# A decoder block on one core: softmax rows divided by VectorE, bias rows fetched from GpSimd's queue, and the sums of down's weights moved to other stages

## The chip, the core and the metric

The kernel runs on one core of a Trainium2 chip. The core has a matrix engine (TensorE, PE in the profile; its weight loads are a row of their own, PEld), VectorE (DVE), ScalarE (ACT), GpSimd (POOL) and SyncE (SP). Each works through a queue of its own in order and waits on semaphores for the others. Transfers are issued from the queues of SyncE, ScalarE and GpSimd. The metric is the device time of one execution in microseconds (us), the median of several runs; a single profiled execution gives the trace.

## The reference

One layer of a decoder block for 512 tokens of width 1024, all in float32:

```python
h = rms_norm(x, norm1_g) * (1 + scale1) + shift1          # shift, scale, gate = silu(c) @ ada_w + ada_b
q, k, v, p, g_attn, g_pool = split(h @ w_in)
q, k = rms_norm(heads(q)), rms_norm(heads(k))             # 8 heads of 64
attn = softmax(q @ k.T / 8 + bias[h, distance], causal) @ v
pool = (multiscale_pool(p) @ pool_w) * pool_scale         # trailing means over 2, 4, 8, 16 tokens
merged = sigmoid(g_attn) * (attn @ w_branch_attn) + sigmoid(g_pool) * (pool @ w_branch_pool)
x = x + gate1 * (merged @ w_out)
h2 = rms_norm(x, norm2_g) * (1 + scale2) + shift2
u_g, u_v = split(causal_dwconv3(h2 @ w_up))               # 2 x 2816 channels
x = x + gate2 * ((silu(u_g) * u_v) @ w_down)
```

With 512 tokens, blocks of 256 and three blocks to choose, the sparse attention selects every past block, so it is plain causal attention. The bias depends on the distance of query and key alone.

## The kernel before

**Precision.** Every float32 factor is split into a rounded part and a remainder (`hi`, `lo`: a ScalarE copy, then a VectorE subtraction), and each product is three matmuls (`mm3`, lines 131 to 134): hi by hi, hi by lo, lo by hi. So a weight tile of 128x1024 that arrives by DMA (`load_unit`, L81, a ring of five tiles issued by SyncE) costs one ScalarE copy (L113) and one VectorE subtraction (L123 or L1043) before TensorE can use it; `ahead` does this two units in advance.

**Order.** The queues of TensorE, VectorE and ScalarE run in the order of the program text. SyncE's and GpSimd's are ordered by the framework's planner, by the program's order and by when a tile's memory is free. Most tiles are 128x512 and come from one pool of 72 slots.

**Stages, in the order in which they run.** x is normalised and transposed; p and q, then k and v are projected; the eight heads run with the sixteen gate projections between them; the branches (A for attention, B for pooling, merged by the sigmoids of the gates); out; up with its convolution, 22 pairs of channel tiles; down.

**The heads (lines 785 to 808).** TensorE alternates: transposes of head h's softmax rows (`flip`, PT), logits of head h + 1 (S, L592 and L593), five steps of a gate, stacks of Q or K for a later head (T, L549), values of head h (O, L644), then more gate steps. Around it, in program order:

- `logits(h + 1)`: VectorE adds the bias to S and takes the row minimum in one pass (L601) for the four query tiles of 512, 384, 256 and 128 keys; ScalarE takes the exponential with the row sum (L605). The bias tile `trev` (128x512) is fetched from a small table `fd` in DRAM, row p shifted by p (`trev_get`, L578, ScalarE's queue). The fetch for head h + 1 is issued behind the exponentials of head h.
- `softmax`: VectorE's reciprocal (L616), then ScalarE multiplies the row tile by it (L617).
- `stacks`: ScalarE and VectorE in turn copy and split Q or K (L556, L557, L564, L565).
- `values`: ScalarE's `bot` (L651) and VectorE's `at` (L652) add the halves of O.
- `ada_col(2, h)` and `ada_col(3, h)`: one VectorE pass each over a 128x1024 tile (L206) for one column of a modulation vector.
- `t_get(h)` and `t_do(h - 1)`: see below.
- the splits of the gates' weights and of PT (L218, L219); O needs PT_l, the remainder of PT.

`pooling(3)` stands in head 5, its ScalarE split (`pool_h`, L218) in front of the evacuation of the next gate (L499).

**The sums of down's weights.** Down is done with seven products in place of eight, which need four sums of the weight blocks b11, b12, b22, b21. They are made ahead, in eleven sets kk = 0 to 10: `t_load` fetches four 128x512 blocks (L756, SyncE), `t_forms` adds them with four VectorE instructions (L761 to L764) and stores the four sums to DRAM (`tsum`, L766, GpSimd's queue), from where down loads them (`raw_t`). Sets 0 to 6 are added in heads 1 to 7, set 7 in the branches (L848), set 8 at pair 2 of up, sets 9 and 10 at pairs 20 and 21 (`T_AT`, L1132).

**Branches and out.** For j = 0 to 7: the branch weights (`br`), B and A, the sigmoids, `mg` = merged split by L218 and L219, and the split of out's weights, whose remainders GpSimd subtracts (L219, `wo_l`). Out adds to x per token tile t: `out_post` (L896, L897, with x fetched by GpSimd, L888), `out_norm` (L191 to L907, `xn`), transposes `hT` (L870), then h2 split into `h2h` and `h2l` (L877 to L880).

**Up.** The first four weight tiles run in two halves of the tokens (lines 1134 to 1141). `h_forms` makes sums of h2 for the pairs in `SEVEN` (even pairs 4 to 18), which also use seven products; the others use `up_mm`. `behind(0)` is the convolution of the pair before (L944 to L946), `behind(1)` its silu and product (L960, L967). `ka`, `kb`, `wg` (L1108) are ScalarE copies that TensorE waits for before it goes on in the same bank. `ada_col(5, k)` stands at the eight pairs of `ADA_AT`.

Of the kernel before, what the change touches and what calls it, by code (L numbers as in the profile page):

```python
# [15 lines left out]
P = 128  # L16
S = 512
D = 1024
H = 8
# [36 lines left out]
def block_kernel(tc, x, cvec, ada, wtok, wch, pool_w, wbr, wout, wup, wdn, pack, table, out):  # L56
# [4 lines left out]
    with ctx:  # L61
# [11 lines left out]
        def slot(name, dt=F32, w=512):  # L73
            return sp.tile([P, w], dt, tag="s", name=name)
# [494 lines left out]
        ath, atl = [], []  # L569
        apair = {}  # L570

        trevs = {}

        def trev_get(h):

            trevs[h] = slot(f"trev_{h}")
            fsrc = fd[h : h + 1, :]
            nc.scalar.dma_start(  # L578
                trevs[h], bass.AP(tensor=fsrc.tensor, offset=fsrc.offset, ap=[[1, P], [1, 512]]))

        def logits(h):

            ta = trevs.pop(h)[:, :]
            pss = []
            for qt in (3, 2, 1, 0):
                n = max((qt + 1) * P, 256)
                if qt:
                    sb = bank(f"S_{h}_{qt}")
                    sps = sb
                else:  # L590
                    sps = sb[:, 256:]
                nc.tensor.matmul(sps[:, :n], Q[h][:, tslice(qt)], K2[h][:, :n], start=True, stop=False)  # L592
                nc.tensor.matmul(sps[:, :n], Q[h][:, tslice(qt)], K1[h][:, :n], start=False, stop=True)  # L593
                pss.append(sps)
            rows, sms = [], []
            for i, qt in enumerate((3, 2, 1, 0)):
                n = (qt + 1) * P
                L = slot(f"L_{h}_{qt}")
                mn = mini.tile([P, 1], F32, tag="mn", name=f"mn_{h}_{qt}")
                rev = bass.AP(tensor=ta.tensor, offset=ta.offset + n - 1, ap=[list(ta.ap[0]), [-1, n]])  # L600
                nc.vector.tensor_tensor_reduce(  # L601
                    out=L[:, :n], in0=pss[i][:, :n], in1=rev, op0=ALU.add, op1=ALU.min, scale=1.0,
                    scalar=3e38, accum_out=mn)
                sm = mini.tile([P, 1], F32, tag="sm", name=f"sm_{h}_{qt}")
                nc.scalar.activation(L[:, :n], L[:, :n], AF.Exp, scale=-1.0, bias=mn, accum_out=sm)  # L605
                rows.append(L)
                sms.append(sm)
            if h + 1 < H:
                trev_get(h + 1)
            return rows, sms  # L610

        def softmax(h, rows, sms):
            for i, qt in enumerate((3, 2, 1, 0)):
                n = (qt + 1) * P
                ri = mini.tile([P, 1], F32, tag="ri", name=f"ri_{h}_{qt}")
                nc.vector.reciprocal(ri, sms[i])  # L616
                nc.scalar.activation(rows[i][:, :n], rows[i][:, :n], AF.Copy, scale=ri)  # L617
            return rows[::-1]


# [84 lines left out]
        fill(kgen, 3)  # L705
        pooling(0)
        pooling(1)
        fill(kgen, 4)
        qn = head_norm(qps, qr, "q")
        fill(kgen, 4)  # L710
# [3 lines left out]
        fill(kgen, 1)  # L714
        for g in range(2):
            pool_proj(g)
        fill(kgen, 3)
        fill(kgen, 2)
        fill(kgen, 100)
# [3 lines left out]
        vps = [bank(f"v_{t}") for t in range(TT)]  # L723
        vgen = tok_proj(2, vps, "v")
        fill(vgen, 3)
        fill(vgen, 4)
        kn = head_norm(kps, kr, "k")
        fill(vgen, 1)
        stacks(0, True)
        fill(vgen, 2)  # L730
        trev_get(0)
        stacks(1, True)
        stacks(0, False)
        fill(vgen, 5.5)
        rows = logits(0)
        fill(vgen, 2)
# [19 lines left out]
                nc.sync.dma_start(b[nm], wdn[plain[nm], i][:, u * 512 : u * 512 + 512])  # L756
            return b

        def t_forms(kk, b):
            i, u = divmod(kk, 2)  # L760
            nc.vector.tensor_add(b["b11"], b["b11"], b["b12"])  # L761
            nc.vector.tensor_add(b["b12"], b["b12"], b["b22"])
            nc.vector.tensor_add(b["b22"], b["b22"], b["b11"])
            nc.vector.tensor_add(b["b21"], b["b21"], b["b22"])  # L764
            for n, nm in (("t1", "b11"), ("t3", "b12"), ("t2", "b22"), ("t4", "b21")):
                nc.gpsimd.dma_start(tsum[n, i][:, u * 512 : u * 512 + 512], b[nm])  # L766

        tb = {}

        def t_get(kk):  # L770
            tb[kk] = t_load(kk)

        def t_do(kk):
            t_forms(kk, tb.pop(kk))

        gates = {}

# [7 lines left out]
        for h in range(H):  # L785
            pt = flip(h, rows)
            if h + 1 < H:
                rows = softmax(h + 1, *logits(h + 1))
            fill(gg, 3)
            if h % 2 == 0 and h < 6:  # L790
                stacks(h // 2 + 1, False)
            elif h in (1, 3):
                stacks((h + 3) // 2, True)
            values(h, *pt)
            ada_col(2, h)
            t_get(h)
            if h:
                t_do(h - 1)
            if h == 5:
                pooling(3)  # L800
            if h == 6:
                pool_proj(3)

            fill(gg, 3 if h < 5 else (share - 3) / 2)
            if h < 5:
                ada_col(3, h)
            fill(gg, (share - 3) / 2)
# [17 lines left out]
        for j in range(8):  # L825
# [18 lines left out]
            a, b = split_act(gp, f"mg_{j}")  # L844
            mgh.append(a)
            mgl.append(b)
            if j == 1:
                t_do(7)  # L848
            if j == 6:
                g1 = row_of(2, "g1")  # L850

# [57 lines left out]
        for t in range(TT):  # L909
            for f in range(2):  # L910
                if (t, f) == (0, 0):
                    for t_ in range(2):
                        for f_ in range(2):
                            out_mm(t_, f_, 0, KT - 2)
                if (t, f) != (3, 0):
                    out_mm(t, f, KT - 2 if t < 2 else 0, KT)
                    out_post(t, f, ops[t, f])
                if late:
                    ada_col(4, late.pop(0))
                    if not late:  # L920
                        nc.vector.scalar_tensor_tensor(acol[:, 32:40], acol[:, 32:40], 1.0, pk[:, C_N2 : C_N2 + 8],
                                                       op0=ALU.add, op1=ALU.mult)
            out_norm(t)
            if t == 2:
                out_mm(3, 0, 0, KT)
                out_post(3, 0, ops[3, 0])
                flip_h2(1)
# [200 lines left out]
            keep(ug[:, R], X)  # L1128
            return ug, uv

        ADA_AT = [4, 6, 8, 10, 12, 14, 16, 18]
        T_AT = [2, 20, 21]  # L1132
        first = []
        for i in range(4):
            ahead(f"up{i}", min(2, 2 * PLAIN - 1 - i))
            first.append((ready.pop(f"up{i}"), bank(f"u_{i}")))
            up_mm(first[i][1], first[i][0], 0, 256)
            if i == 1:
                flip_h2(3)
        for w, ps in first:  # L1140
            up_mm(ps, w, 256, 512)
        pend, summed = [], []
        S_AT = [3, 7, 11, 18]

# [13 lines left out]
        for j in range(NP):  # L1158
# [24 lines left out]
                behind(1)  # L1183
            pend.append((j, *u))
            if j + 1 in T_AT:
                t_get(8 + T_AT.index(j + 1))
            if j in T_AT:
                t_do(8 + T_AT.index(j))
            for k in range(8):
                if ADA_AT[k] == j:  # L1190
                    ada_col(5, k)
        behind(0)
        behind(1)


        g2 = row_of(5, "g2")
# [167 lines left out]
```

## Time and profile before

| | us |
|---|---|
| median of 3 runs (lowest, highest) | 701.92 (701.43, 702.06) |
| profiled execution | 704.26 |
| its span, first to last instruction | 702.0 |

Stages in the trace (us from the span's start): the heads with the gates about 109 to 252, branches 252 to 303, out 303 to 348, up 348 to 590, down to the end. In the profile's rows, "out<-in" are the tiles written and read, L123 is a line, and the text after "<-" in brackets names what ended the idle time of that engine. Times of a stretch are busy times of each engine; the granted clock is that of TensorE, 1.00 for full speed.

### The profile page before, as it was taken

What the parts mean: (1) busy time and instruction counts of PE and PEld (TensorE: products, weight loads), DVE (VectorE), ACT (ScalarE), POOL (GpSimd) and SP (SyncE); (2) the same over time, 40 slices, a digit from 0 to 9 for tenths busy, and PEclk for the clock granted to TensorE, in tenths of its full rate; (3) what the DMA queues carried; (4) which work ended last, traced back from release to release, by engine and by line L of the source; (5) the groups of instructions that cost most, each with busy time, mean ns of one, the idle gap of its engine ahead of it and who ended that gap; (6) DMA issues with size and microseconds to landing.
All of it is one profiled execution on the core that took longest, in us unless ns stands there. A gap on an engine that the chain in (4) does not pass through costs nothing.

```text
span 702.0 us, 9585 instructions
## 1 busy us (share of the span) xinstructions
PE 667.8 (95%) x3403; PEld 566.2 (81%) x3403; DVE 562.2 (80%) x922; ACT 380.7 (54%) x663; POOL 88.0 (13%) x117
## 2 busy tenths in 40 slices
PE   8999999988896897999999899999999999999997
PEld 6778788867675786788897789998889988788885
DVE  7887866676767779886659999898998897978774
ACT  8454546756663744640555555565655643867430
POOL 2003120011111134461300100000000011001000
PEclk9999999999999899999999999999999999999999
DMA  8875232666667499678323444234243397577751
GB/s 351 312 262 187 92 106 89 200 243 216 235 239 262 166 211 264 229 228 312 136 89 107 150 142 128 101 141 150 90 145 127 124 218 263 184 237 261 249 189 59
DMA packets 41830, 131.52 MB, mean 187 GB/s; under 512 B 5315, under 2 KB 5484, under 8 KB 41782
## 3 DMA queue, kind: packets, MB, share of 16 engines
q1 hardware_dynamic: 34694, 109.77, 45.7%
q0 software_dynamic: 5936, 19.04, 9.1%
q10 hardware_dynamic: 1152, 2.10, 0.8%
q8 instruction: 26, 0.43, 0.2%
q14 instruction: 22, 0.18, 0.1%
HBM read 115.13 MB, written 15.76 MB: 186 GB/s over the span
## 4 chain that ended last, share of the span: by engine, by line
PE 66%; DVE 17%; ACT 9%; issue 5%; DMA 2%; SPq 0%; ACTq 0%; DVEq 0%
PE u L133 6%; PE u L132 6%; PE u L134 6%; DVE raw_ada L206 3%; PE X L139 2%; PE X L140 2%; PE X L138 2%; PE uX L138 2%; PE uX L140 2%; PE uX L139 2%; PE o L134 2%; PE o L133 2%; PE o L132 2%; DMA raw_p<-in_wtok 2%; ACT L L605 2%
## 5 line engine op out<-in xcount | busy, mean ns | idle before, releaser
L132 PE MATMUL u<-h2h,hi_up 128*128 128x512 f32 (+1 forms) x256 | 93.1, 364 | 1.0 <-ACT hi_up L113 1.0
L134 PE MATMUL u<-h2h,lo_up 128*128 128x512 f32 (+1 forms) x256 | 92.9, 363 | 0.5 <-DVE lo_up L1043 0.5
L133 PE MATMUL u<-h2l,hi_up 128*128 128x512 f32 (+1 forms) x256 | 92.9, 363 | 0.0
L206 DVE CUSTOM_DVE_ANT_0 raw_ada<-raw_ada,cbc,pk 128x1024 f32<-128x1024 f32 x48 | 61.7, 1294 | 4.9 <-DMA raw_ada<-in_ada 2.8
L132 PEld LDWEIGHTS u<-h2h,hi_up 128*128 128x128 f32 x256 | 48.4, 189 | 8.7 <-ACT hi_up L113 1.4
L134 PEld LDWEIGHTS u<-h2h,lo_up 128*128 128x128 f32 x256 | 48.3, 189 | 8.5 <-DVE lo_up L1043 1.0
L133 PEld LDWEIGHTS u<-h2l,hi_up 128*128 128x128 f32 x256 | 48.4, 189 | 7.1
L132 PE MATMUL gate_ps<-h_h,hi_gate 128*128 128x512 f32 x128 | 52.1, 407 | 0.0
L133 PE MATMUL gate_ps<-h_l,hi_gate 128*128 128x512 f32 x128 | 51.6, 403 | 0.0
L134 PE MATMUL gate_ps<-h_h,lo_gate 128*128 128x512 f32 x128 | 51.6, 403 | 0.0
L766 POOL DMA_DIRECT2D tsum_t<-b x44 | 24.0, 546 | 205.2 <-DVE b L761 200.1
L605 ACT ACTIVATE L<-L,mn 128x512 f32<-128x512 f32 (+3 forms) x32 | 17.6, 551 | 33.5 <-DVE mn L601 21.0
L113 ACT ACTIVATE hi_t<-raw_t 128x1024 fp32r<-128x1024 f32 (+1 forms) x24 | 23.7, 988 | 17.5 <-PE Y L140 8.4
L123 DVE TENSOR_TENSOR lo_t<-raw_t,hi_t 128x1024 fp32r<-128x1024 f32 (+1 forms) x24 | 26.6, 1131 | 8.0 <-ACT hi_t L113 7.9
L113 ACT ACTIVATE hi_up<-raw_up 128x1024 fp32r<-128x1024 f32 x28 | 29.3, 1049 | 4.3 <-PE u L133 4.3
L1043 DVE TENSOR_TENSOR lo_up<-raw_up,hi_up 128x1024 fp32r<-128x1024 f32 x22 | 26.8, 1220 | 3.7 <-ACT hi_up L113 3.7
L134 PEld LDWEIGHTS gate_ps<-h_h,lo_gate 128*128 128x128 f32 x128 | 25.1, 196 | 5.6
L132 PEld LDWEIGHTS gate_ps<-h_h,hi_gate 128*128 128x128 f32 x128 | 25.5, 199 | 4.9
L133 PEld LDWEIGHTS gate_ps<-h_l,hi_gate 128*128 128x128 f32 x128 | 25.3, 198 | 4.9
L219 POOL TENSOR_TENSOR wo_l<-raw_wo,wo_h 128x512 fp32r<-128x512 f32 x16 | 25.0, 1580 | 19.9 <-ACT wo_h L218 17.6
L113 ACT ACTIVATE hi_b<-raw_b 128x1024 fp32r<-128x1024 f32 (+1 forms) x18 | 17.7, 984 | 13.6 <-PE X L140 8.1
L132 PE MATMUL o<-wo_h,mg_h 128*128 128x512 f32 x64 | 25.0, 391 | 0.0
(357 smaller groups left out, 1976.2 us busy)
## 6 DMA issues: line engine op xcount, KB each, us to landing
raw_ada<-in_ada SPq DMA_DIRECT2D x48, 512.0 KB, 4.7
raw_up<-in_wup SPq DMA_DIRECT2D x44, 512.0 KB, 3.3
b<-in_wdn SPq DMA_DIRECT2D x44, 256.0 KB, 5.2
tsum_t<-b POOLq DMA_DIRECT2D x44, 256.0 KB, 3.4
raw_t<-tsum_t SPq DMA_DIRECT2D x20, 512.0 KB, 4.4
raw_gate<-in_wch SPq DMA_DIRECT2D x16, 512.0 KB, 3.9
raw_b<-in_wdn SPq DMA_DIRECT2D x15, 512.0 KB, 7.8
raw_br<-in_wbr SPq DMA_DIRECT2D x8, 512.0 KB, 4.8
```

Source lines behind the costliest of these rows:

```text
L113: nc.scalar.activation(hi, raw, AF.Copy)
L123: nc.vector.tensor_sub(lo, raw, hi.bitcast(F32))
L132: nc.tensor.matmul(ps, sh, mh, start=start, stop=False)
L133: nc.tensor.matmul(ps, sh, ml, start=False, stop=False)
L134: nc.tensor.matmul(ps, sl, mh, start=False, stop=stop)
L138: nc.tensor.matmul(ps, sh, mh, start=start, stop=False, skip_group_check=True)
L139: nc.tensor.matmul(ps, sh, ml, start=False, stop=False, skip_group_check=True)
L140: nc.tensor.matmul(ps, sl, mh, start=False, stop=stop, skip_group_check=True)
L206: nc.vector.tensor_tensor_reduce(out=raw, in0=raw, in1=cbc, op0=ALU.mult, op1=ALU.add, scale=1.0, scalar=col(C_AB + i), accum_out=acol[:, ...
L219: (eng or nc.vector).tensor_sub(lo[:, :w], src, hi[:, :w].bitcast(F32))
L605: nc.scalar.activation(L[:, :n], L[:, :n], AF.Exp, scale=-1.0, bias=mn, accum_out=sm)
L1043: nc.vector.tensor_sub(lo, raw, hi.bitcast(F32))
```

## The change

Four things, in the diff below.

1. `trev` is allocated and fetched at the head of `logits(h)` for its own head, from GpSimd's queue; the fetch behind the exponentials of the head before is gone.
2. The softmax rows are multiplied by the reciprocal on VectorE (`tensor_scalar`) and no longer on ScalarE.
3. The sets of sums move: 0 and 1 are loaded in heads 6 and 7 and added in branches j = 0 and 1; 2 and 3 are loaded in out at t = 0 and 1 and added at t = 1 and 2; 4 is loaded at t = 2 and added after the second tile of up's first four; 5 to 10 are added at pairs 0, 2, 6, 10, 20 and 21. Adding and storing are separate functions now (`t_do`, `t_put`), and the stores are issued from ScalarE's queue: sets 0 and 1 at branches j = 2 and 3, set 2 and 3 between up's first tiles, set 4 behind them, the others one pair after their sums.
4. Of the eight `ada_col(5, k)`, four move from up to the projections of k and v; four stay, at pairs 4, 8, 12 and 16.

```diff
-        def trev_get(h):
-            trevs[h] = slot(f"trev_{h}")
-            fsrc = fd[h : h + 1, :]
-            nc.scalar.dma_start(
-                trevs[h], bass.AP(tensor=fsrc.tensor, offset=fsrc.offset, ap=[[1, P], [1, 512]]))
         def logits(h):
-            ta = trevs.pop(h)[:, :]
+            trev = slot(f"trev_{h}")
+            fsrc = fd[h : h + 1, :]
+            nc.gpsimd.dma_start(
+                trev, bass.AP(tensor=fsrc.tensor, offset=fsrc.offset, ap=[[1, P], [1, 512]]))
+            ta = trev[:, :]
...
-            if h + 1 < H:
-                trev_get(h + 1)
             return rows, sms
...
                 nc.vector.reciprocal(ri, sms[i])
-                nc.scalar.activation(rows[i][:, :n], rows[i][:, :n], AF.Copy, scale=ri)
+                nc.vector.tensor_scalar(rows[i][:, :n], rows[i][:, :n], ri, None, op0=ALU.mult)
...
         pooling(1)
+        ada_col(5, 0)
         fill(kgen, 4)
...
             pool_proj(g)
+        ada_col(5, 1)
...
         fill(vgen, 3)
+        ada_col(5, 2)
...
-        trev_get(0)
         stacks(1, True)
         stacks(0, False)
+        ada_col(5, 3)
...
+        def t_do(kk):
+            b = tb[kk]
             nc.vector.tensor_add(b["b11"], b["b11"], b["b12"])
             nc.vector.tensor_add(b["b12"], b["b12"], b["b22"])
             nc.vector.tensor_add(b["b22"], b["b22"], b["b11"])
             nc.vector.tensor_add(b["b21"], b["b21"], b["b22"])
+        def t_put(kk):
+            i, u = divmod(kk, 2)
+            b = tb.pop(kk)
             for n, nm in (("t1", "b11"), ("t3", "b12"), ("t2", "b22"), ("t4", "b21")):
-                nc.gpsimd.dma_start(tsum[n, i][:, u * 512 : u * 512 + 512], b[nm])
+                nc.scalar.dma_start(tsum[n, i][:, u * 512 : u * 512 + 512], b[nm])
...
             ada_col(2, h)
-            t_get(h)
-            if h:
-                t_do(h - 1)
+            if h > 5:
+                t_get(h - 6)
...
             mgl.append(b)
-            if j == 1:
-                t_do(7)
+            if j < 2:
+                t_do(j)
+            elif j < 4:
+                t_put(j - 2)
...
             out_norm(t)
+            if t < 3:
+                t_get(2 + t)
+            if 0 < t < 3:
+                t_do(1 + t)
...
-        ADA_AT = [4, 6, 8, 10, 12, 14, 16, 18]
-        T_AT = [2, 20, 21]
+        ADA_AT = {4: 4, 8: 5, 12: 6, 16: 7}
+        T_AT = [0, 2, 6, 10, 20, 21]
...
             up_mm(first[i][1], first[i][0], 0, 256)
+            if i < 2:
+                t_put(2 + i)
             if i == 1:
                 flip_h2(3)
+                t_do(4)
+                t_get(5)
         for w, ps in first:
             up_mm(ps, w, 256, 512)
+        t_put(4)
...
             if j + 1 in T_AT:
-                t_get(8 + T_AT.index(j + 1))
+                t_get(5 + T_AT.index(j + 1))
             if j in T_AT:
-                t_do(8 + T_AT.index(j))
-            for k in range(8):
-                if ADA_AT[k] == j:
-                    ada_col(5, k)
+                t_do(5 + T_AT.index(j))
+            if j - 1 in T_AT:
+                t_put(5 + T_AT.index(j - 1))
+            if j in ADA_AT:
+                ada_col(5, ADA_AT[j])
         behind(0)
         behind(1)
+        t_put(10)
```

More of the change, by code (lines that the diff above doesn't have):

```diff
@@ L570, in block_kernel, with logits @@
         apair = {}
-        trevs = {}
-        def trev_get(h):
-            trevs[h] = slot(f"trev_{h}")
+        def logits(h):
+            trev = slot(f"trev_{h}")
             fsrc = fd[h : h + 1, :]
-            nc.scalar.dma_start(
-                trevs[h], bass.AP(tensor=fsrc.tensor, offset=fsrc.offset, ap=[[1, P], [1, 512]]))
-        def logits(h):
-            ta = trevs.pop(h)[:, :]
+            nc.gpsimd.dma_start(
+                trev, bass.AP(tensor=fsrc.tensor, offset=fsrc.offset, ap=[[1, P], [1, 512]]))
+            ta = trev[:, :]
             pss = []
@@ L757, in t_load, with t_get @@
             return b
-        def t_forms(kk, b):
-            i, u = divmod(kk, 2)
+        tb = {}
+        def t_get(kk):
+            tb[kk] = t_load(kk)
+        def t_do(kk):
+            b = tb[kk]
             nc.vector.tensor_add(b["b11"], b["b11"], b["b12"])
@@ L764, in t_forms @@
             nc.vector.tensor_add(b["b21"], b["b21"], b["b22"])
+        def t_put(kk):
+            i, u = divmod(kk, 2)
+            b = tb.pop(kk)
             for n, nm in (("t1", "b11"), ("t3", "b12"), ("t2", "b22"), ("t4", "b21")):
[L766 to L774, printed above, removed]
+                nc.scalar.dma_start(tsum[n, i][:, u * 512 : u * 512 + 512], b[nm])
         gates = {}
```

## The prediction, made before the changed kernel was run

> **What bounds the kernel now.** I read the page first (busy shares and clock), then the waits of TensorE, then stretches and the timeline around each wait. The profiled execution took 704.26 us: 702.0 us of span and 2.26 us around it. The median of the three runs is 701.92 us. I make the sum against 704.26 and move the result down by the 2.34 us between the two.
>
> ```profile
> PE 667.8 (95%) x3403; PEld 566.2 (81%) x3403; DVE 562.2 (80%) x922; ACT 380.7 (54%) x663; POOL 88.0 (13%) x117
> ...
> PEclk9999999999999899999999999999999999999999
> ```
>
> TensorE is 95% busy and nearly always at full clock, so a change to another engine pays only where TensorE stands still or runs slowly. Which work it waits for is in its waits (who waited for whom, total us, times, longest):
>
> ```profile
> PE O L644 <- DVE PT_l L219: 10.9, 4, 3.5
> PE S L592 <- ACT gate L499: 6.2, 1, 6.2
> PE B L134 <- DVE lo_br L123: 4.7, 2, 4.3
> PE uX L138 <- ACT ka L1108: 1.9, 1, 1.9
> ...
> PE X L139 <- DVE lo_b L123: 1.6, 1, 1.6
> PE u L132 <- ACT hi_up L113: 1.0, 1, 1.0
> PE u L134 <- DVE lo_up L1043: 0.5, 1, 0.5
> ```
>
> The first two rows, 17.1 us, lie in the heads' loop; the third in the branches; the others in up and at the start of down. A wait also costs clock afterwards. The stretches below give us, busy time of PE, PEld, DVE, ACT and POOL with their counts, granted clock, DMA share and GB/s:
>
> ```profile
> 137.20:155.90 18.70, 15.28 (x79) 12.84 (x79) 13.96 (x30) 10.82 (x23) 2.27 (x4) 1.00 0.67 241
> 137.20:146.06 8.86, 8.86 (x41) 7.39 (x42) 4.92 (x17) 5.96 (x15) 0.00 (x0) 1.00 0.79 291
> 155.89:166.40 10.51, 10.51 (x42) 8.67 (x43) 5.09 (x17) 8.01 (x19) 0.00 (x0) 0.84 0.65 243
> 174.70:178.10 3.40, 3.40 (x17) 2.94 (x18) 2.74 (x12) 1.83 (x7) 0.00 (x0) 1.00 0.99 360
> 227.60:234.40 6.80, 4.42 (x12) 3.66 (x13) 4.96 (x9) 4.85 (x8) 0.00 (x0) 0.57 0.18 56
> 401.70:405.10 3.40, 3.27 (x18) 3.27 (x19) 3.40 (x5) 2.25 (x6) 0.00 (x0) 0.64 0.24 77
> ```
>
> Rows two and three are the same work of two heads (from the start of O to the transposes): 8.86 us at full clock, 10.51 at 0.84 after a wait of 3.4 us, so 1.65 us more. The first row is a whole head: TensorE needs 15.28 us of its 18.70. Why the rest is lost shows in one head's timeline (start, us, engine, line):
>
> ```profile
> 186.46 0.69 DVE L761 TENSOR_TENSOR b<-b,b 128x512 f32<-128x512 f32 x1
> ...
> 189.25 1.22 DVE L123 TENSOR_TENSOR lo_gate<-raw_gate,hi_gate 128x1024 fp32r<-128x1024 f32 x1
> ...
> 193.46 0.50 PE L644 MATMUL O<-PT_h,v 128*128 128x512 f32 x1 [3.50 <-DVE PT_l L219]
> ...
> 197.23 1.91 ACT L617 ACTIVATE L<-L,ri 128x512 f32<-128x512 f32 x4
> ...
> 199.04 1.36 ACT L564 ACTIVATE K<-T_False,pk 64x512 fp32r<-64x512 f32 x2
> ```
>
> VectorE runs its program in order: bias, softmax, K stacks, `at`, a modulation sum, the four sums of down (186.46 to 189.25, 2.8 us), gate splits, then PT_l, for which O waits. ScalarE divides the rows (1.91 us) before it makes the K stacks that VectorE waits for. The two make one ring of 18.7 us with no TensorE work in it; TensorE needs 15.3.
>
> **The change part by part.** *Heads: sums leave, division moves.* The ring loses 2.8 us of sums and 1.9 us of division: 18.7 - 2.8 - 1.9 = 14.0 us. The divisions on VectorE are priced by a scaling of the same shape:
>
> ```profile
> L904 DVE TENSOR_SCALAR xn<-x,rs_y x8: 479/484/487, 330.7 to 353.2; 128x512 f32<-128x512 f32 x8
> ```
>
> Four rows of 512, 384, 256 and 128 columns cost at most 4 x 0.48 = 1.9 us, by width about 1.2. Each follows its own reciprocal while ScalarE is still in the next exponential, and the last ends under ScalarE's first two K stacks (1.36 us), so I charge the ring nothing; without that cover it is 14.0 + 1.9 = 15.9, 0.6 over TensorE. At 14.0 the ring is 1.3 us faster than TensorE, so the four waits of O (10.9) go, and with them two slow stretches of 1.6: 14.1.
>
> The 6.2 us wait for a bank is the pooling in head 5:
>
> ```profile
> 228.68 0.63 ACT L218 ACTIVATE pool_h<-pool 128x512 fp32r<-128x512 f32 x1 [8.84 <-DVE pool L676]
> ```
>
> ScalarE stands in front of that split while the gate's evacuation, which frees the bank, queues behind it. The evacuation would come 2.8 + 1.9 us earlier, and some 2 us more because VectorE then leads O instead of trailing it (the four waits above are 2.7 us on the mean): 6.7 in all against 6.2. So it goes, with about 2 us of slow clock (0.57 over the 6.80 us stretch, 4.42 of them busy). Heads: 14.1 + 6.2 + 2 = **-22.3**. Late next is TensorE itself.
>
> *Bias rows fetched from POOL.* Their issue and landing, beside the issues of the sums' loads and stores:
>
> ```profile
> L578 ACTq DMA_DIRECT2D trev<-fd x8: 326/327/349, 95.9 to 214.8; - x8
> ```
> ```profile
> trev<-fd ACTq DMA_DIRECT2D x8, 256.0 KB, 5.3
> ```
> ```profile
> L756 SPq DMA_DIRECT2D b<-in_wdn x44: 327/383/628, 121.0 to 574.8; - x44
> L766 POOL DMA_DIRECT2D tsum_t<-b x44: 539/540/636, 149.9 to 586.8; - x44
> ```
>
> The eight issues leave ScalarE (0.33 us each, under its activations) and cost POOL 0.54 each. In the heads POOL's queue holds nothing else once the stores are gone, so a fetch waits only for its slot and should land well ahead of its head: 0. Its price if it doesn't is a rival below. [...]
>
> *Four modulation sums beside k and v* (costliest groups: busy us, mean ns, idle before):
>
> ```profile
> L206 DVE CUSTOM_DVE_ANT_0 raw_ada<-raw_ada,cbc,pk 128x1024 f32<-128x1024 f32 x48 | 61.7, 1294 | 4.9 <-DMA raw_ada<-in_ada 2.8
> ```
>
> 1.3 us each. TensorE's waits name no tile of k or v, so its k and v products cover them: 0; one sum, 1.3, if that cover is short.
>
> *Branches.* Two sets of sums stood ahead of the row of br that TensorE waits for (head 7 and j = 1); two still do (j = 0 and j = 1). The 4.3 us stay. New are eight stores on ScalarE between `mg_h` and the next `hi_br`, on which `lo_br` depends: 4 x 0.33 = 1.3 us a set, nothing if issued under an activation, 2 if they go like four loads of SP. I take 0.75 a set: **+1.5**.
>
> *Out.* Two sets come into VectorE's queue, 5.6 us, ahead of `h2l` and of the last `xn`. VectorE's own waits from 336 to 369 us tell what absorbs them:
>
> ```profile
> DVE lo_up L123 <- ACT hi_up L113: 4.8, 2, 3.1
> DVE h2l L880 <- ACT h2h L879: 3.6, 8, 0.5
> DVE x L897 <- DMA x<-in_x: 3.2, 3, 1.5
> ```
> The timelines of VectorE and of TensorE at the last of them:
>
> ```profile
> 352.84 0.88 DVE L904 TENSOR_SCALAR xn<-x,rs_y 128x512 f32<-128x512 f32 x2 [0.68 <-POOL rs_y L197]
> ```
> ```profile
> 353.95 0.82 PE L870 MATMUL hT<-pk,xn 128*128 128x128 f32 x6
> ```
>
> The waits for x (3.2) take it up in part, 2.4 are left; xn is ready 0.2 us before hT takes it: **+2.2** (0 if all is absorbed, 5.6 if nothing). The third set comes where VectorE waits 3.1 us for `hi_up`: 0.
>
> *Up's head.* The set at j = 0 stands where VectorE is the bound (TensorE's waits for `hi_up` and `lo_up`, 1.5 us): 2.8 in full, and the stores put ahead of the next `hi_up` 1.0 more. That wait becomes 5.3 us and so brings a slow stretch (1.6). The slow stretch delays TensorE by 1.6 but not VectorE and ScalarE, so the wait for `ka` (1.9) shrinks by 1.6, less the 1.0 of four more stores ahead of it: 0.6 back. Together **+4.8**. [...]
>
> *Rest of up.* The sets at j = 6 and 10 replace modulation sums (1.3 us), those at 14 and 18 are gone: +1.5 us twice on VectorE. TensorE's one wait for `uX` is that at 401.70; behind it no pair of up waits, so the products cover this. Stores at j = 7 and 11 stand ahead of `ka`, where ScalarE has time:
>
> ```profile
> ACT ka L1108 <- PE uX L140: 11.4, 7, 2.3
> ```
>
> 1.6 us each: 0, at most 6.
>
> *Tail.* The last four stores come before a `hi_b` on which the 1.6 us wait for `lo_b` depends: **+1.0**, from 0 to 3.4 with a slow stretch.
>
> Sum: -22.3 + 1.5 + 2.2 + 4.8 + 1.0 = -12.8; 704.26 - 12.8 = 691.5 for a profiled execution, **689 us** for the median.
>
> **The rivals.**
> 1. *All sums hidden*: the places of out, up's head and tail absorb them. For it speaks VectorE's idle time; against it that VectorE is the last to end in up's head. 701.92 - 22.3 + 1 = 681.
> 2. *The division stays in the ring*: 15.9 against 15.3 us, 0.6 a head over four heads and about 1 at the pooling: 689 + 3.5 = 692.5.
> 3. *Up turns VectorE-bound*: sets at j = 6 and 10 or stores there make TensorE wait, 3 us and a slow stretch of 1.6 each: 689 + 9 = 698. Against it: no later pair waits now, and four sums leave.
> 4. *Late bias rows, slower than before*: the fetch stands directly ahead of its use in the program, no longer a head ahead; if POOL issues it only then, VectorE waits the 5.3 us of landing in every head. Less the ring's 1.3 us that is 4.0, with slow clock 5.6 a head; six heads 34: 689 + 34 = 723. It decides from 12.8 / 6 = 2.1 us of wait a head, a landing 3.4 us after need. The three waits for x in out (3.2 us) are fetches that POOL got to late, behind work of its own; in the heads it has none, which speaks against it. [...]
>
> **How the numbers follow.** Forecast 0.55, rivals 0.12, 0.12, 0.13 and 0.08 in order. The forecast's unknown costs reach from 681 (as rival 1) to some 696; with rival 3 the range is 681 to 698, leaving out rival 4 and part of the ends. Faster by over 0.2% (about what a measurement of this kernel can tell from no change) are the forecast, rivals 1 and 2 and most of rival 3: 0.89. Within 0.2%: 0.03. Slower: 0.08.
>
> **What would show it.** The waits of O for PT_l and of S for a bank gone; O to O at 15.3 us; B's wait for `lo_br` near 4 us still there; a longer wait for `hi_up` near the start of up (5 us) and some 2 us before hT; the bias L601 never behind a DMA. Wrong would be: O still waiting (ring not shortened), L601 waiting for the fetch, or new waits in up's later pairs.

## The result, and the profile after

| | before | changed |
|---|---|---|
| median of 4 runs (lowest, highest), us | 701.67 (701.28, 702.06) | 692.94 (692.15, 693.36) |
| profiled execution, us | 704.26 | 692.15 |
| its span, us | 702.0 | 690.4 |

The ratio is 0.9874, 95% interval 0.9857 to 0.9891: 8.7 us faster. The forecast was 689, from 681 to 698.

The page of the changed kernel, busy time and granted clock:

```profile
PE 663.9 (96%) x3403; PEld 563.1 (82%) x3403; DVE 571.8 (83%) x954; ACT 367.0 (53%) x631; POOL 69.5 (10%) x81
...
PEclk9999999999999998999998999999999999999999
```

VectorE has taken over 9.6 us of work, ScalarE has lost 13.7. What TensorE waits for now (who waited for whom, total us, times, longest):

```profile
PE B L134 <- DVE lo_br L123: 5.4, 3, 4.4
PE u L132 <- ACT hi_up L113: 5.2, 1, 5.2
PE B L132 <- ACT hi_br L113: 3.0, 1, 3.0
PE uX L138 <- ACT ka L1112: 2.1, 3, 1.3
...
PE hT L870 <- DVE xn L904: 1.0, 1, 1.0
PE T_True L549 <- DVE n_k L527: 0.5, 1, 0.5
```

No wait for PT_l or for a bank is left: the heads are free. In their place stand a longer wait for `hi_up`, a new one for `hi_br`, and small ones for `xn`, `n_k` and `ka`. The stretches of two whole heads and of the time behind four waits (us, then busy time of PE, PEld, DVE, ACT, POOL, granted clock, DMA share, GB/s):

```profile
137.75:152.80 15.05, 15.05 (x82) 12.85 (x80) 13.36 (x37) 9.96 (x22) 0.55 (x1) 1.00 0.49 169
152.80:167.85 15.05, 15.05 (x81) 12.85 (x80) 12.51 (x30) 10.48 (x23) 0.55 (x1) 1.00 0.55 179
255.57:258.97 3.40, 3.40 (x8) 2.67 (x9) 2.95 (x5) 0.42 (x1) 0.00 (x0) 0.53 0.70 242
271.83:275.23 3.40, 2.87 (x7) 2.05 (x8) 3.37 (x4) 2.03 (x4) 1.82 (x2) 0.64 0.97 317
372.65:376.05 3.40, 3.36 (x7) 2.25 (x8) 3.33 (x5) 2.89 (x5) 0.00 (x0) 0.50 0.51 169
376.05:378.60 2.55, 2.55 (x7) 1.97 (x7) 2.55 (x5) 1.02 (x2) 0.00 (x0) 0.50 0.19 74
391.05:394.45 3.40, 3.40 (x28) 3.40 (x29) 2.35 (x4) 2.83 (x5) 0.00 (x0) 1.00 1.04 314
```

A head takes 15.05 us, all of them TensorE's. Rows three to five are slow clock behind waits of 4.4, 3.0 and 5.2 us; the sixth continues the fifth, so behind the 5.2 us wait the clock stayed at half for 6.0 us. The last is full clock behind the 1.3 us wait for `ka`.

The next table is worked out from the traces: from the start of TensorE's first instruction of one kind to that of the next, in us. "Only division" and "only the rest" are the first two experiments, "single" and "placed" two later ones.

| stage | before | changed | only division | only the rest | single | placed |
|---|---|---|---|---|---|---|
| k and v (first k to first T) | 34.04 | 34.68 | 34.04 | 34.69 | 34.70 | 34.71 |
| heads (first PT to first B) | 137.06 | 112.24 | 123.50 | 123.23 | 112.20 | 112.24 |
| branches (to the first o) | 50.45 | 56.36 | 49.09 | 56.22 | 51.06 | 47.16 |
| out (to the first u) | 45.33 | 45.33 | 45.33 | 45.33 | 45.33 | 45.33 |
| up's head (to pair 4, first uX) | 48.69 | 56.20 | 48.69 | 56.13 | 54.43 | 51.27 |
| pairs 4 and 5 | 24.62 | 22.59 | 24.62 | 22.58 | 21.57 | 20.98 |
| rest of up (to the first X) | 168.62 | 169.84 | 168.62 | 169.97 | 168.62 | 168.62 |
| down | 111.88 | 111.29 | 111.59 | 111.29 | 114.54 | 111.26 |

The change wins 24.8 us in the heads and gives back 13.3: 0.6 beside k and v, 5.9 in the branches, 5.5 from up's head to pair 5, 1.2 behind it. Another 0.5 is lost ahead of the first k, before anything that moved (over all runs, that k starts at 59.4 to 60.8 us); down gains 0.6.

### The profile page after: what moved, and what is told of

It reads as the page before. It is cut to its first block, busy times and chain, and to the rows that moved or that the text cites. A ratio compares the mean times of both kernels' runs of the same rounds, so it can differ in the third digit from the quotient of the medians.

```text
span 690.4 us, 9511 instructions
## 1 busy us (share of the span) xinstructions
PE 663.9 (96%) x3403; PEld 563.1 (82%) x3403; DVE 571.8 (83%) x954; ACT 367.0 (53%) x631; POOL 69.5 (10%) x81
## 4 chain that ended last, share of the span: by engine, by line
PE 56%; DVE 18%; issue 13%; DMA 7%; ACT 3%; POOL 2%; SPq 1%; DVEq 0%; POOLq 0%; ACTq 0%
PE u L133 4%; PE u L132 4%; PE u L134 4%; DMA raw_p<-in_wtok 3%; PE gate_ps L134 3%; PE gate_ps L133 3%; PE gate_ps L132 3%; PE X L139 3%; PE X L140 2%; PE X L138 2%; DVE raw_ada L206 2%; PE o L133 2%; PE o L132 2%; PE o L134 2%; PE uX L138 2%
## 5 line engine op out<-in xcount | busy, mean ns | idle before, releaser
L132 PE MATMUL gate_ps<-h_h,hi_gate 128*128 128x512 f32 x128 | 50.0, 390 | 0.0
L134 PE MATMUL gate_ps<-h_h,lo_gate 128*128 128x512 f32 x128 | 50.0, 390 | 0.0
L133 PE MATMUL gate_ps<-h_l,hi_gate 128*128 128x512 f32 x128 | 49.9, 390 | 0.0
L113 ACT ACTIVATE hi_t<-raw_t 128x1024 fp32r<-128x1024 f32 (+1 forms) x24 | 23.7, 987 | 17.5 <-PE Y L140 8.4
L219 POOL TENSOR_TENSOR wo_l<-raw_wo,wo_h 128x512 fp32r<-128x512 f32 x16 | 24.8, 1570 | 31.6 <-ACT wo_h L218 31.6
L132 PEld LDWEIGHTS gate_ps<-h_h,hi_gate 128*128 128x128 f32 x128 | 24.0, 188 | 4.6
L134 PE MATMUL o<-wo_h,mg_l 128*128 128x512 f32 x64 | 24.9, 389 | 0.0
```

The costliest lines, as they stand in the source:

```text
L113: nc.scalar.activation(hi, raw, AF.Copy)
L132: nc.tensor.matmul(ps, sh, mh, start=start, stop=False)
L133: nc.tensor.matmul(ps, sh, ml, start=False, stop=False)
L134: nc.tensor.matmul(ps, sl, mh, start=False, stop=stop)
L219: (eng or nc.vector).tensor_sub(lo[:, :w], src, hi[:, :w].bitcast(F32))
```

## The experiments

All times are medians; before is 702.0 to 702.9 us in the runs beside them. Expectations speak of the changed kernel's 692.94 us.

**1. The change without the division.**

```diff
-                nc.vector.tensor_scalar(rows[i][:, :n], rows[i][:, :n], ri, None, op0=ALU.mult)
+                nc.scalar.activation(rows[i][:, :n], rows[i][:, :n], AF.Copy, scale=ri)
```

> The changed kernel with the softmax division back on ScalarE, and nothing else. By the forecast's ring (18.7 less 2.8 of sums = 15.9 us; a head of TensorE's takes 15.05 in the trace of the changed kernel) each head waits up to 0.85 us: 0 to 5 in all, about 1 more at the pooling in head 5: about 697. Rival: the sums alone freed the heads, and the division is hidden on either engine: 693. Second rival: the division is most of it, since it stood between the exponentials and the K stacks that VectorE waits for: 700 and more.

704.34 us, ratio 1.0042 (1.0027 to 1.0058): slower than before. TensorE's waits in the heads are back, and a head's stretch shows the ring:

```profile
PE S L587 <- ACT gate L499: 3.4, 1, 3.4
PE O L637 <- DVE PT_l L219: 2.5, 4, 0.7
```
```profile
155.47:171.39 15.92, 15.40 (x78) 12.86 (x78) 10.59 (x25) 11.55 (x24) 0.55 (x1) 1.00 0.44 140
```

From O to O it takes 15.92 us; the forecast's sum for a ring without the sums of down was 15.9. The ring reading holds. The median is 7 us above the 697 expected, and the heads are 11.0 us longer than the changed kernel's. What the expectation missed is head 5 with the pooling: 21.7 us from O to O against 15.3 in the changed kernel, 6.4 more where I had put 1.

**2. The division alone.** The same line the other way round, in the kernel before.

> The kernel before with the division on VectorE, and nothing else: the sums stay in the heads. By the ring (18.7 - 1.9 = 16.8 us against 15.05 to 15.3 of TensorE) the four waits of O fall from 10.9 us to about 6 and their slow stretches (3.2) go, the wait for a bank in head 5 falls by about 2: 10 us less, 692 us. Rival: VectorE has no room for the division beside the sums, it only moves from one engine of the ring to the other, 1.2 to 1.9 us: 700 to 702. Second rival: the division alone is what freed the heads: 680.

688.89 us, ratio 0.981 (0.9797 to 0.9823), 3 us below the 692 expected. One line of the diff does more than the whole diff. Its waits and the last of its ordinary heads:

```profile
PE O L644 <- DVE PT_l L219: 4.3, 3, 1.9
...
PE S L592 <- ACT gate L499: 2.9, 1, 2.9
```
```profile
184.70:201.64 16.94, 15.06 (x75) 12.53 (x75) 14.54 (x33) 9.74 (x20) 2.16 (x4) 1.00 0.76 256
```

The ring was forecast at 16.8 and measures 16.94 here; the heads ahead of it still draw on a lead of VectorE (15.05, 15.05, 16.0). Experiments 1 and 2 with the two kernels make a table of four: the division takes 13.6 us from the heads (137.06 to 123.50), the absence of the sums 13.8 (to 123.23), both 24.8 (to 112.24). Each part pays there. But the sums had to go somewhere: with the division in place, the rest of the change wins 11.3 in the heads and loses 14.6 ahead of and behind them. Experiments 8 and 9 leave little of that to the bias rows and the modulation sums.

**3. Additions left out.** The body of `t_do` is empty, loads and stores stay, so down gets unsummed blocks.

```diff
         def t_do(kk):
-            b = tb[kk]
-            nc.vector.tensor_add(b["b11"], b["b11"], b["b12"])
...
+            pass
```

> The changed kernel without the 44 additions on VectorE; the loads and the stores stay, so down gets unsummed blocks (a part of the computation is left out). It prices what the additions cost at their new places, apart from the stores. If the branches' 4.39 us wait for lo_br with its slow clock is owed to them it goes (5.7), in out the 0.96 of hT goes (1.2), in up's head the sums of set 5 go from VectorE but the stores ahead of hi_up stay (2.8 less and, the wait of 5.16 being 2.4 then, a slow stretch still): about 10 less, 683. Rival: the stores on ScalarE are what all the waits come from, the additions lie beside TensorE's work everywhere: 690 to 693. Second rival: VectorE is the bound of up's pairs too: 678.

678.57 us, 4 below the 683 expected. By stages: branches 48.21 (8.2 less), from up's head to pair 5 76.47 (2.3 less), rest of up 168.62 (1.2 less). What stays is:

```profile
PE B L132 <- ACT hi_br L113: 2.7, 1, 2.7
PE u L132 <- ACT hi_up L113: 2.3, 1, 2.3
PE hT L866 <- DVE xn L900: 1.9, 1, 1.9
...
PE B L134 <- DVE lo_br L123: 1.0, 2, 0.5
```

The long wait for `lo_br` was the additions' (4.4, now 0.5). The wait for `hi_up` fell by 2.8 us, the length of one set, to 2.3. The wait for `hi_br` is not owed to additions, but here the clock stayed at 1.00 behind it (265.04 to 268.44), which is part of why the branches gave more than the 5.7 expected.

The wait of `hT` for `xn` did not go: it is 1.9 us with no sum ahead of it and 1.0 in the changed kernel. What VectorE waits for in out is the fetch of x: 9.0 us here, 3.1 with the sums, and 2.07 and 1.38 of these just ahead of that `xn`. So the sums of out lie in time that VectorE waits anyway. This wait, and half clock for 6.5 us behind the wait for `hi_up`, leave up's head only 0.7 us shorter (55.49).

The median is near the second rival's 678, but its mechanism is not there: up as a whole gave 3.5, the branches most. The runs of this kernel spread from 675.1 to 680.3, the profiled one being the longest, so I read it by stages.

**4. Stores from GpSimd's queue.**

```diff
-                nc.scalar.dma_start(tsum[n, i][:, u * 512 : u * 512 + 512], b[nm])
+                nc.gpsimd.dma_start(tsum[n, i][:, u * 512 : u * 512 + 512], b[nm])
```

> The changed kernel (692.94 us) with the 44 stores of the sums issued from GpSimd's queue, at the same places of the program, and not from ScalarE's. If the issues on ScalarE are what the branches lost (5.9 us from the start of B to the start of out, where 1.5 was forecast) and part of what up lost, the branches keep only the wait for lo_br that was there before: 5.7 us less; up's head 1.3 less (the wait for hi_up ends when ScalarE is through with the copies of the h sums), the pairs 7 and 11 1.2 less: about 685. Rival: the sums on VectorE cost it, whatever queue stores them: 692 to 693. Second rival: a store from GpSimd holds up the wo_l subtractions there and VectorE's two-input instructions beside them: above 693.

688.74 us, ratio 0.9807 (0.9791 to 0.9823): half of what was expected. Its waits:

```profile
PE B L134 <- DVE lo_br L123: 6.3, 3, 5.6
PE u L132 <- ACT hi_up L113: 3.8, 1, 3.8
PE u L133 <- DVE h2l L880: 3.1, 1, 3.1
```

`hi_br` and `ka` are waited for no longer and the `hi_up` wait is 1.4 shorter, so these were ScalarE's. New is a wait for `h2l`: on GpSimd's queue three stores at 314.39 now stand ahead of a fetch of x (316.37), VectorE waits 2.67 us for that x, and `h2l` is queued behind it. Why the `lo_br` wait grew by 1.2 I did not settle.

**5. Stores one at a time, still on ScalarE.** `t_put` only notes its four stores; `drip` issues one, and stands behind each sigmoid, each split of out's weights, each convolution's first activation and each silu.

```diff
+        def drip():
+            if due:
+                nc.scalar.dma_start(*due.pop(0))
...
             nc.scalar.activation(gp, gp, AF.Sigmoid)
+            drip()
             nc.scalar.activation(ga, ga, AF.Sigmoid)
+            drip()
```

> The changed kernel with the stores still on ScalarE, but one at a time: each behind a sigmoid, a split of out's weights, a convolution's first activation or a silu, and no four in a row. In the changed kernel the four issues of a set take 0.33, 0.44, 0.47 and 0.5 to 1.3 us. If it is the row of four that costs, a single one takes 0.33 us as the fetches of trev did and hides under the activation ahead of it: branches 5 us less, up's head 1.3 to 2 less, pairs 7 and 11 1.2 less: about 685. Rival: the length of an issue comes from what the transfer engines have to do at the time (a DMA share of 0.9 to 1.0 in the branches) and not from the row; then single ones take up to 1.3 us too, and half of the loss stays: about 689.

685.65 us, ratio 0.9766 (0.9746 to 0.9786), as expected. ScalarE's timeline in the changed kernel at branches 2 and 3 shows what a row costs (start, us, engine, line; the ACTq rows are the issues):

```profile
258.55 0.63 ACT L218 ACTIVATE mg_h<-gate 128x512 fp32r<-128x512 f32 x1 [6.66 <-DVE gate L841]
258.56 2.45 ACTq L773 DMA_DIRECT2D tsum_t<-b  x4
261.11 1.06 ACT L113 ACTIVATE hi_br<-raw_br 128x1024 fp32r<-128x1024 f32 x1 [1.93 <-issue]
...
267.92 0.63 ACT L218 ACTIVATE mg_h<-gate 128x512 fp32r<-128x512 f32 x1 [3.67 <-DVE gate L841]
267.93 2.67 ACTq L773 DMA_DIRECT2D tsum_t<-b  x4
270.72 1.06 ACT L113 ACTIVATE hi_br<-raw_br 128x1024 fp32r<-128x1024 f32 x1 [2.16 <-issue]
```

Four issues take 2.45 and 2.67 us. The first hides under `mg_h`, the others hold ScalarE for 1.93 and 2.16 us, and `hi_br`, for which TensorE waits, comes that much later. The same place with single stores:

```profile
257.85 0.63 ACT L224 ACTIVATE mg_h<-gate 128x512 fp32r<-128x512 f32 x1 [6.66 <-DVE gate L850]
257.98 0.34 ACTq L110 DMA_DIRECT2D tsum_t<-b  x1
258.38 1.04 ACT L119 ACTIVATE hi_br<-raw_br 128x1024 fp32r<-128x1024 f32 x1
258.38 0.93 ACTq L110 DMA_DIRECT2D tsum_t<-b  x2
259.33 0.61 ACT L832 ACTIVATE gate<-gate 128x512 f32<-128x512 f32 x1
259.37 1.03 ACTq L110 DMA_DIRECT2D tsum_t<-b  x1
```

The four issues still follow each other closely and are about as long as in the row (0.34, 0.42, 0.44 and 1.03 us against 0.34, 0.45, 0.48 and 1.08). What differs is their place: only the first stands ahead of `hi_br`, and the others run under `hi_br` and the sigmoids.

The issues of all 44 stores, shortest, median and longest ns, changed kernel first, then this one:

```profile
L773 ACTq DMA_DIRECT2D tsum_t<-b x44: 326/464/1310, 258.6 to 580.7; - x44
```
```profile
L110 ACTq DMA_DIRECT2D tsum_t<-b x44: 326/327/1623, 258.0 to 572.4; - x44
```

Over the whole kernel the median falls from 464 to 327 ns. In the branches the rival is right about the length: with the transfer engines' share at 0.86 to 1.02, some issues of this kernel took 0.8 to 1.6 us too. But activations that others wait for lay ahead of them, which is what counted: branches 5.3 less, rest of up 1.2 less. The tail is 3.2 worse: the last stores were left over and went out in a row ahead of a `hi_b`.

**6. Set 5 away from up's head.**

```diff
-        T_AT = [0, 2, 6, 10, 20, 21]
+        T_AT = [2, 6, 10, 14, 20, 21]
...
                 t_do(4)
-                t_get(5)
```

> The changed kernel with set 5 loaded at pair 1 .. and added at pair 14: sets 5 to 8 are added at pairs 2, 6, 10 and 14 in place of 0, 2, 6 and 10, each stored one pair later. By the forecast's term for up's head (4.8 us, from 2.8 of sums, 1.0 of stores and a slow stretch), the 5.16 us wait of u for hi_up falls to about 1.5 and the slow stretch behind it goes, the wait of uX for ka gets 0.6 longer: about 688.5. Rival: behind 400 us VectorE has nearly no idle time (0.1 to 0.2 us of each 10), so the set at pair 14 costs what it saved at pair 0: 691 to 693.

689.74 us, ratio 0.9827 (0.9807 to 0.9848). The wait for `hi_up` is back to 1.0, up's head at 49.82 us, 6.4 less. But pairs 4 and 5 take 27.17, 4.6 more:

```profile
PE uX L138 <- ACT ka L1112: 4.7, 3, 3.8
```
```profile
387.06:390.46 3.40, 3.40 (x16) 3.40 (x17) 1.53 (x2) 1.60 (x4) 0.00 (x0) 0.50 0.93 293
```

The `ka` wait of 1.3 is now 3.8 and followed by half clock. I read it so: VectorE and ScalarE are the bound until pair 4; an earlier wait of TensorE gives them time, and without it they are late at the next place. The rival had the place wrong (the rest of up, with pair 14, is 0.4 longer), and so had I.

**7. Set 0 added in head 7, set 1 in branch 0, none in branch 1.**

```diff
-            if h > 5:
-                t_get(h - 6)
+            if h in (5, 6):
+                t_get(h - 5)
+            if h == 7:
+                t_do(0)
...
-            if j < 2:
-                t_do(j)
+            if j == 0:
+                t_do(1)
```

> The changed kernel with set 0 loaded in head 5 and added in head 7, where VectorE has 6 us of idle time (220 to 230 us), and set 1 loaded in head 6 and added in branch 0; branch 1 has no set. If the 4.39 us wait of B for lo_br is owed to a set of sums and a modulation sum in a row at branches 0 and 1, it goes with its slow stretch of 1.6: about 687. Rival: the wait comes from VectorE's instructions running at double length beside GpSimd's subtractions (lo_br 2.27 us for 1.22), and one set in branch 0 is enough for it: about 691 to 693.

691.34 us, ratio 0.9847 (0.9831 to 0.9863). Branches 52.95, 3.4 less:

```profile
PE B L134 <- DVE lo_br L123: 2.5, 3, 1.4
```

The wait for `lo_br` falls from 4.4 to 1.4, still there with one set. VectorE's timeline at branch 1 of the changed kernel shows the other half of it:

```profile
250.95 0.69 DVE L765 TENSOR_TENSOR b<-b,b 128x512 f32<-128x512 f32 x1
251.68 1.63 DVE L766 TENSOR_TENSOR b<-b,b 128x512 f32<-128x512 f32 x1
253.24 2.28 DVE L123 TENSOR_TENSOR lo_br<-raw_br,hi_br 128x1024 fp32r<-128x1024 f32 x1
```

An addition of 0.69 takes 1.63, and `lo_br` 2.28 for its 1.22, while GpSimd's two `wo_l` subtractions run (251.45 to 254.43): a set of sums there costs 2.8 and 2 more for the company (without the additions, in experiment 3, `lo_br` takes 1.2 us in every branch). Both of my readings were half right. Of the 3.4 won, 1.4 went in up's head, where the waits for `h2l` and `xn` are 1.3 and 0.9 longer, and 1.2 in pairs 4 and 5; what set that off is not settled.

**8. The bias rows from ScalarE again**, one head ahead, as before.

```diff
-            nc.gpsimd.dma_start(
-                trev, bass.AP(tensor=fsrc.tensor, offset=fsrc.offset, ap=[[1, P], [1, 512]]))
+            nc.scalar.dma_start(
+                trevs[h], bass.AP(tensor=fsrc.tensor, offset=fsrc.offset, ap=[[1, P], [1, 512]]))
...
+            if h + 1 < H:
+                trev_get(h + 1)
```

> The changed kernel with the bias rows fetched as before: from ScalarE's queue, one head ahead. The forecast has the move at 0 (the fetch is hidden in either place, a single issue of 0.33 us lies under an activation): 692.3 to 693.6. Rival: ScalarE loses 0.33 us a head in a ring that is close to TensorE: up to 695. Rival on the other side: the fetch from GpSimd's queue lands late in some head and the changed kernel is the slower one: below 692.

692.40 us (691.84 to 692.73): no difference that can be measured. Issue and landing from GpSimd in the changed kernel:

```profile
L576 POOL DMA_DIRECT2D trev<-fd x8: 546/546/632, 95.5 to 199.3; - x8
```
```profile
trev<-fd POOLq DMA_DIRECT2D x8, 256.0 KB, 3.6
```

**9. The four modulation sums back in up.**

```diff
-        ada_col(5, 0)
...
-        ADA_AT = {4: 4, 8: 5, 12: 6, 16: 7}
+        ADA_AT = {4: 0, 6: 1, 8: 2, 10: 3, 12: 4, 14: 5, 16: 6, 18: 7}
```

> The changed kernel with its four modulation sums taken from the projections of k and v and put back to the pairs 4, 6, 8, 10 in up (the other four at 12, 14, 16, 18, as before). The trace of the changed kernel has a wait of 0.49 us of T for n_k in the projections that was not there (0.65 us with its slower clock), and TensorE comes to the heads 1.18 us later than before, of which 0.53 arose at 37.65 us, ahead of anything that was moved. So the projections should give 0.65 back; up's pairs have VectorE nearly without idle time and take 4 x 1.3 us more: 0 if TensorE's products cover it, as before, so about 692.3; rival: with sets of sums at pairs 6 and 10 as well up turns bound by VectorE, and waits of up to 1.3 us a pair come up: 694 to 697.

693.31 us: no difference that can be measured. The projections win back 0.65 us (34.04), up's later pairs lose 2.6 (172.41) in two waits for `ka` of 1.6 and 1.7 (0.4 each in the changed kernel): the rival's waits, but at two pairs only.

**10. The sums spread.** Sets 0 and 1 as single additions in the heads, set 2 at the start of out, set 3 at its second tile, sets 5 to 8 at pairs 2, 6, 10, 14; stores single, behind weight copies too.

```diff
-            if h > 5:
-                t_get(h - 6)
+            if h in (0, 3):
+                t_get(h // 3)
+            for n in {1: (0,), 2: (1,), 3: (2,), 4: (3,), 5: (4,), 6: (5,), 7: (6, 7)}.get(h, ()):
+                t_one(n // 4, n % 4)
...
+        t_do(2)
+        t_get(3)
...
-        T_AT = [0, 2, 6, 10, 20, 21]
+        T_AT = [2, 6, 10, 14, 20, 21]
```

> The changed kernel (692.94 us) with the sums spread over the room that the runs show: sets 0 and 1 added one addition a head (heads 1 to 6, two in head 7), whose ring would be 14.0 + 0.7 = 14.7 us against 15.05 of TensorE; set 2 at the start of out, set 3 at its second tile, set 4 as it was, sets 5 to 8 at pairs 2, 6, 10 and 14, and every store single, behind an activation (weight copies too). Stage by stage: heads unchanged at 112.2; branches without any set about 46 (56.4 in the changed kernel, 51.1 with single stores alone); up to the first seven-product pair 48.7 (56.2); the rest as with single stores, the tail back to 111.3: about 675. Rival: an addition in each head brings the waits of O back (up to 0.7 a head): 680. Second rival: up's later pairs, where VectorE has no idle time left, take what up's head gives: 680 to 684.

687.65 us, ratio 0.9785 (0.9767 to 0.9804). A miss: 675 was expected. Heads 116.1:

```profile
PE u L140 <- DVE h2l L897: 2.9, 1, 2.9
...
PE B L139 <- ACT hi_br L119: 2.2, 1, 2.2
PE S L594 <- ACT gate L506: 2.0, 1, 2.0
```

The ordinary heads bore an addition (15.05 us from O to O), head 5 with the pooling did not (19.1). In the branches eight stores went out within 14 us, beside the loads. Two loads of `br` landed 11.4 and 10.2 us after their issue, and one `hi_br` came 1.5 us late for that; but the changed kernel has a `br` that took 10.6 us, so what made TensorE wait 2.2 us for the next `hi_br` is not settled. In out, `h2l` stood behind a wait of VectorE for x of 1.65 us, at a place where the changed kernel has none.

**11. Placed by what the runs showed.** Single stores, in rows of four only for the last two sets; sets 0 and 1 both in head 7, set 0 ahead of the values; none in the branches; sets 5 to 10 at pairs 6, 10, 14, 18, 20 and 21.

```diff
+            if h == 7:
+                t_do(0)
             values(h, *pt)
             ada_col(2, h)
-            if h > 5:
-                t_get(h - 6)
+            if h in (5, 6):
+                t_get(h - 5)
+            if h == 7:
+                t_do(1)
...
-        T_AT = [0, 2, 6, 10, 20, 21]
+        T_AT = [6, 10, 14, 18, 20, 21]
```

> The changed kernel with single stores (behind activations, four in a row only for the last two sets), sets 0 and 1 both added in head 7 (set 0 ahead of the values, where VectorE waits 3.67 us for O in the run with set 0 in head 7; set 1 where set 0 was there), none in the branches, and sets 5 to 10 at pairs 6, 10, 14, 18, 20 and 21, so that none is at pairs 0 and 2. Stage by stage, from the runs: to the heads' end as in the changed kernel (112.2 for the heads); branches 48 (51.1 with single stores alone, less the 4.39 us wait for lo_br and its slow clock, plus what the loads cost); up to the first product of pair 4 in its seventh step 70.1 (76.0 with single stores, less the waits of 3.79 and 0.52 for hi_up and lo_up and a slow stretch of 1.6); the tail 111.3: about 674. Rival: sets at pairs 14 and 18 cost what pairs 0 and 2 give, since up is bound by VectorE as a whole: 680. Second rival: the 8 loads of sets 0 and 1 in heads 5 and 6 or the sums in head 7 delay the start of the branches: 677 to 680.

675.41 us (673.53 to 676.06), ratio 0.9605 (0.9578 to 0.9632): the fastest, 17.5 us below the change as it was made. Its largest waits in total, and its branches, up's head and pairs 4 and 5 by stretches:

```profile
PE X L145 <- DVE lo_b L129: 1.6, 1, 1.6
PE xT L289 <- DVE wm L169: 1.5, 1, 1.5
PE B L138 <- ACT hi_br L119: 1.4, 2, 0.8
```
```profile
229.54:276.70 47.16, 44.71 (x194) 35.74 (x193) 39.51 (x46) 27.94 (x45) 21.15 (x14) 1.00 0.64 219
322.03:373.31 51.28, 47.67 (x306) 42.62 (x305) 43.01 (x71) 29.62 (x50) 2.19 (x4) 1.00 0.34 118
373.31:394.29 20.98, 20.98 (x134) 19.09 (x133) 20.52 (x31) 13.24 (x24) 0.00 (x0) 1.00 0.57 189
```

No wait is over 1.6 us and the clock is 1.00 in all three.

## Why the prediction was right, and where not

Right in direction and within its range, 3.9 us low. Against the profiled execution it forecast -12.8; the two profiled executions stand 12.1 apart. Most of the 3.9 is the step that took 2.34 us off as if each kernel's profile stood that far above its median: that of the changed kernel stands 0.8 below. The sum itself came out by luck, mainly from misses of opposite sign: the branches were 4.4 us worse than forecast, the rest of up 1.2, k and v 0.6; the heads were 2.5 better, the tail 1.6, out 1.0.

- **Heads, -22.3: measured -24.8.** The mechanism, a ring of ScalarE and VectorE that loses 2.8 and 1.9 us, is shown by experiments 1 and 2 (15.92 and 16.94 measured, 15.9 and 16.8 forecast). Mis-sized was the pooling's head, 8.2 forecast (6.2 and 2 of clock): from O to O it went from 26.7 to 15.3 us, 11.5. Of these 2.1 are the fourth wait of O, counted among the 10.9, so 9.4 stand against the 8.2; half clock lasted 5.4 us behind the wait for the bank. Rival 2's 3.5 us, for a division left in the ring, is 11.0 in the heads, 6.4 of it in the pooling's head.
- **Divisions at nothing: right.** They take 487, 420, 361 and 286 ns on the mean by width (1.55 us a head), and the heads run at TensorE's 15.05.
- **Bias rows at 0: right** (experiment 8). No fetch was late: the eight issues took 546 to 632 ns, and the three that ran beside a division of VectorE took 546.
- **Modulation sums beside k and v at 0:** +0.64, half of the bound given (1.3).
- **Branches, +1.5: measured +5.9. This is the step that failed.** The 4.3 us for `lo_br` stayed, as forecast. The stores were priced at 0.75 us a set, by four single issues of 0.33. Four in a row hold ScalarE 1.9 and 2.2 us; the second row made TensorE wait 3.0 and brought a slow stretch (0.64). Single stores gave 5.3 us back: shown by experiment 5.
- **Out, +2.2:** 0 up to the first u, then 1.0 at hT and 0.2 behind it. The place was right and the mechanism wrong: without the sums that wait is 1.9, and VectorE's wait ahead of it is for x (experiment 3). The forecast left 2.4 us of sums that no wait for x takes up; the runs show them absorbed. Why x lands later than in the kernel before is not shown.
- **Up's head, +4.8: +4.3, right in its waits and in part by luck.** The wait forecast at 5.3 is 5.2; the sums' 2.8 and the stores' 1.0 measure 2.8 (experiment 3) and 1.4 (experiments 4 and 5). The slow stretch behind it, put at 1.6, was half clock for 6.0 us and cost about 2.7: of the 6.3 us that up's head grew apart from hT, 4.1 are more wait for `hi_up`, less 0.5 of wait for `lo_up`. From the first u to the end of pair 5 it is +5.5, of which 1.2 is hT's. Against that the `ka` stretch, pairs 4 and 5, gives back 2.0 and not 0.6: the wait ended at 1.3 us without a slow stretch (1.00). I had left in the slow stretch that stood behind this wait before, when it was 1.9 us. The length alone did not tell: waits of 1.9 us went both ways in the trace of before, to 0.64 (`ka`, 401.70:405.10) and to 1.00 (PT_l, 174.70:178.10).
- **Rest of up, 0: +1.2**, two waits for `ka` (pairs 8 and 12) of 0.36 each and as much behind them. They are gone without the additions (experiment 3) as well as with the stores elsewhere (4 and 5), so it takes the sums and the row of stores together. **Tail, +1.0: -0.6**; the wait for `lo_b` is 1.6 as before.

Rival 1 (all sums hidden) was wrong for the change as made, yet experiment 11 shows that the places for it exist. Rival 3 was right only in small (two waits of 0.4), rival 4 did not occur.

## What to carry to other kernels

Measure the parts of a change alone: here one line was worth 13 us, and the sums' move, good for the heads (11 us), cost more than that at its new places. Work is hidden only where the chain that TensorE waits for has room: test a place by the engine's idle time just ahead of the wait, and expect a shortened wait to show up again at the next place where the same engines are late (in experiment 6 `hi_up` went from 5.2 to 1.0 us and `ka` from 1.3 to 3.8). Issue transfers from a computing engine one at a time, each behind an activation that covers it, and not in a row ahead of one that others wait for (two rows of four held ScalarE 1.9 and 2.2 us ahead of `hi_br`).

## What the runs showed of the hardware

- Of ScalarE's 44 store issues in experiment 5 the median took 0.33 us. In the changed kernel's row of four at branch 2 they took 0.34, 0.45, 0.48 and 1.08 us, and the engine's next activation waited 1.93 us for the last. That row took 2.45 us, with the transfer engines' share at 1.02; the row at 369.66 took 1.83, with the share at 0.55. In experiment 5 some took 0.8 to 1.6 us in the branches, at shares of 0.86 to 1.02.
- In the changed kernel an addition of two tiles on VectorE took 1.63 us for 0.69, and a subtraction 2.28 for 1.22, while GpSimd subtracted tiles beside them (251.45 to 254.43). It was not always VectorE that paid: in the kernel before, at 259.2 us, a `lo_br` kept its 1.22 us and GpSimd's subtraction beside it took 2.16, where most took 1.3 to 1.7.
- After waits of 3.0, 3.8, 4.4 and 5.2 us the granted clock was 0.64, 0.50, 0.53 and 0.50 over the next 3.4 us; after the last it stayed at 0.50 for 6.0 us. The 3.8 is experiment 6, the others are the changed kernel. After 1.3 us it was 1.00. In between both occurred: 0.60 after 2.2 us (experiment 10), 1.00 after 2.5 and 2.7 us (experiments 7 and 3); in the kernel before 0.64 after the 1.9 us wait for `ka` and 1.00 (174.70:178.10) after this one:

```profile
174.69 0.50 PE L644 MATMUL O<-PT_h,v 128*128 128x512 f32 x1 [1.89 <-DVE PT_l L219]
```
